# A hybrid encoder layer: output-projection pieces also in the three preparing turns, and at three quarters of the pace in the turns after them

## The chip, the core and the metric

The kernel runs on one core of a Trainium2 chip. The metric is device time in microseconds (us) of one execution of the whole program. Five engines matter: PE (TensorE, matrix products), DVE (VectorE), ACT (ScalarE), POOL (GpSimd) and SP (SyncE), which here issues every DMA of the program in the order of its own queue. Each engine works through its instructions in a fixed order; an instruction that waits holds everything behind it on the same engine.

## The reference

One post-norm encoder layer over 2048 tokens of width 1024 (batch 1):

```
h = layer_norm(x)
proj = h @ w_in
y = concat(ssd_bidir(proj[...]), rwkv7_bidir(proj[...]))   # 512 + 512 wide
h = layer_norm(ALPHA * h + y @ w_out)                      # the output projection
out = layer_norm(ALPHA * h + square(relu(h @ w_fc)) @ w_proj)
```

The two mixers run over the sequence in both directions. The first one (SSD) is a chunked scan. The second one (RWKV-7) carries a 64 x 64 state per head, updated with a decay, a rank-one removal and a rank-one write for each token:

```
s_kk = einsum('dbhvk,dbhk->dbhv', S, kk)
S = S * w - s_kk[..., None] * (kk * a)[..., None, :] + v[..., :, None] * k[..., None, :]
y = einsum('dbhvk,dbhk->dbhv', S, r)
```

The output projection `y @ w_out` is a sum of two products: the SSD half of `y` with the first 512 rows of `w_out`, and the RWKV half with the last 512 rows. The SSD half is complete before the RWKV scan begins; the RWKV half becomes complete token block by token block as the scan from both ends meets.

## The kernel before, in words

The program has three stages. `phase_in` (line 504) normalises `x`, multiplies it with `w_in` and runs most of the element-wise work and the SSD group. `phase_rwkv` (line 926) runs the RWKV scan. `phase_mlp` (line 1322) is the feed-forward part. Large products are made from three products of split operands (high part times high part, high times low, low times high), so one 128 x 512 output block with 4 chunks of 128 rows costs 12 matmuls.

**The scan.** It is cut into 32 units (`U = 2 * UN`): 16 blocks of 128 tokens for each of two pairs of heads, both directions in one unit. Four generators do the work of a unit.

- `prep(u)` (line 972) loads the unit's tensors (`rk`, `bk0`, `E`: lines 987, 989, 991), scales them (DVE, lines 997 and 999), forms the small products (PE, line 1009), transposes (PE, lines 1023 and 1033), and at its end writes the triangular matrices `at` to memory as `ad` (DMA, line 1040).
- `inverse(u)` (line 1042) loads `ad` back in another layout as `la` (DMA, line 1046), inverts 16 x 16 triangular blocks in 15 steps of two small operations each (lines 1055 and 1056), and changes the layout through memory again (`nd`, line 1059, then `ni`, line 1062). For even units its 30 operations are on DVE, for odd units on POOL.
- `merge(u)` (line 1075) joins the 16 x 16 inverses to 64 x 64 ones with four small products on PE (lines 1092, 1099, 1112, 1120), with DVE and ACT between them (lines 1096, 1103 on DVE, 1106, 1117, 1124 on ACT).
- `chain(u)` (line 1126) is the recurrence itself: for each of two halves three dependent products on PE (all on line 1140: `ch<-zv,kr`, `ch<-rs,nm`, `ch<-zv,bkt`), each followed by a copy on ACT or DVE (lines 1149, 1158, 1159, 1168, 1172, 1175), and the output products (lines 1155, 1182).

**The turns.** The loop at the end of `phase_rwkv` makes one turn per unit, from `u = -3` to 31. In turn `u` it weaves `chain(u)` with `finish(u - 1)`, `merge(u + 1)`, `inverse(u + 2)` and `prep(u + 3)`. The turns -3, -2 and -1 have no chain: there the main line is `iter([None] * 12)`, twelve empty steps, and only `prep`, `inverse` and, in turn -1, `merge(0)` are made.

**The output projection.** `out_pieces` (line 775) is a generator, `k.fill`. It yields `DENSE` after each 3 matmuls of a 128 x 512 output block (line 828), so one token block of 128 has 8 pieces. In order it makes: 8 pieces of gate products for the scan's output (line 866), the loading and splitting of the first 512 rows of `w_out` (DMA line 789, ACT 797, POOL 798), the scale rows of the SSD half (one transpose on line 877, a trip through memory on lines 881 and 811), then for 16 token blocks a load (`h` line 805, `yr` line 808, DVE 813, ACT 815, POOL 817), 8 pieces, two DVE operations that add them to `h` (line 831) and a store of `h` (line 838). Then follow 8 more gate pieces, the other half of `w_out`, and 16 token blocks of the RWKV half (DVE line 833), each of which waits until both scans have passed it and until a given turn.

**What sets the pace.** `dense(ins, n)` (line 1064) is called after each product of `merge` and `chain`. It adds `n` times a rate to a credit and pulls pieces while the credit is at least 1. The rate is `R0` before turn 1, `R1` in turns 1 to 17 and `R2` later. With rates of 1 a turn asks for 8 pieces (4 in `merge`, 4 in `chain`), from turn 17 on for 7. A piece that is pulled there may not be placed ahead of the product after which it was pulled.

```
k.credit += n * (R0 if k.u < 1 else R1 if k.u < 18 else R2)
with tc.issue_after(ins.ins):
    while k.credit >= 1:
        p = next(k.fill, END) if next(k.ssd, END) is END else END
```

The final order on each engine is made by the framework's scheduler, which orders the instructions by their priorities and a timing model of its own.

## Time and profile before

| | us |
|---|---|
| median of 3 runs | 3469.87 |
| lowest, highest | 3465.22, 3473.87 |
| the profiled execution, its own time | 3477.84 |
| its span, first to last instruction | 3476.0 |

One execution was profiled; all numbers of views are from it. The scan begins on PE at about 1034.8 us of the span, when the last product of `phase_in` ends, and its last unit ends at about 1985.5 us. By the ends of the units' last output products (line 1182), unit 0 ends at 1132.6, unit 3 at 1229.8, unit 15 at 1536.7, unit 16 at 1562.4 and unit 31 at 1985.5 us. Over the whole span PE is busy 3162.8 us (91%), DVE 2035.9 (59%), ACT 1240.3 (36%) and POOL 975.8 (28%).

The views give a time from the span's start, a duration in us, the engine, the line, the operation with the names of what it writes and reads, and in brackets the idle time of that engine ahead of it with what ended it. Rows marked SPq are DMA issues on the SP queue.

### The profile page before, as it was taken

The page shows a single profiled execution, that of the slowest core. Times are in us where ns is not written, and L with a number is a line of the kernel's source. Part 1 is how long each engine was busy: PE and PEld are TensorE (multiplying, and loading weights), DVE is VectorE, ACT ScalarE, POOL GpSimd, SP SyncE. Part 2 cuts the span into 40 slices and gives each one's busy share as a digit, 9 for nine tenths or more (in the row PEclk, how much of TensorE's full clock was granted, in tenths as well). Part 3 has the DMA queues.
Part 4 walks back from the last instruction along what each step waited for, and adds up shares of the span by engine and source line. Part 5 has one row for each costly group of instructions (what it writes and reads, how often), then busy time and mean ns, then how long its engine had stood idle before and what let it go on. Part 6 is the DMA issues. An engine that isn't in the chain of part 4 may idle for free.

```text
span 3476.0 us, 62902 instructions
## 1 busy us (share of the span) xinstructions
PE 3162.8 (91%) x24551; PEld 2525.6 (73%) x24551; DVE 2035.9 (59%) x4186; ACT 1240.3 (36%) x2574; POOL 975.8 (28%) x1278
## 2 busy tenths in 40 slices
PE   5879989988876888888898889999999999999998
PEld 4767867766765666666666678888888788888886
DVE  7798457767675666565767554444444664444446
ACT  3556323433335454455655531122222222222221
POOL 0352134444553221223454551111111111111113
PEclk9989999999995899986978999999999999999999
DMA  5345356776777666656665552111111331111111
GB/s 206 132 158 179 122 148 190 210 214 189 214 226 198 158 170 157 161 158 171 171 164 156 151 189 91 49 49 46 47 49 49 103 109 49 49 49 49 49 49 61
DMA packets 630137, 446.70 MB, mean 129 GB/s; under 512 B 193456, under 2 KB 553552, under 8 KB 629840
## 3 DMA queue, kind: packets, MB, share of 16 engines
q1 hardware_dynamic: 629840, 442.69, 43.5%
q8 instruction: 193, 3.16, 0.4%
q14 instruction: 104, 0.85, 0.1%
HBM read 295.43 MB, written 147.14 MB: 127 GB/s over the span
## 4 chain that ended last, share of the span: by engine, by line
PE 58%; DMA 13%; DVE 13%; issue 4%; POOL 3%; SPq 2%; ACT 2%; DVEq 0%; POOLq 0%; ACTq 0%
PE ps L1362 7%; PE ps L1363 7%; PE ps L1364 7%; PE ps L1384 6%; PE ps L1382 6%; PE ps L1383 6%; PE psg L828 3%; DMA R<-rows 2%; PE psg L268 2%; PE psg L269 2%; PE psg L270 2%; PE ch L1140 2%; DMA la<-ad 1%; DMA ad<-at 1%; PE ps L1009 1%
## 5 line engine op out<-in xcount | busy, mean ns | idle before, releaser
L1388 DVE TENSOR_TENSOR acc<-acc,ps 128x512 f32<-128x512 f32 x464 | 318.2, 687 | 445.3 <-PE ps L1384 443.0
L1369 POOL TENSOR_TENSOR ul<-r,uh 128x512 fp32r<-128x512 f32 x128 | 171.1, 1338 | 1189.6 <-ACT uh L1368 1189.6
L1364 PE MATMUL ps<-hl,fh 128*128 128x512 f32 x1024 | 401.6, 392 | 0.0
L1363 PE MATMUL ps<-hh,fl 128*128 128x512 f32 x1024 | 401.5, 392 | 0.0
L1362 PE MATMUL ps<-hh,fh 128*128 128x512 f32 x1024 | 397.5, 393 | 0.6 <-DVE h L833 0.4
L1384 PE MATMUL ps<-ph,ul 128*128 128x512 f32 x1008 | 393.3, 390 | 0.0
L1383 PE MATMUL ps<-pl,uh 128*128 128x512 f32 x1008 | 393.0, 390 | 0.0
L1382 PE MATMUL ps<-ph,uh 128*128 128x512 f32 x1008 | 392.8, 390 | 0.0
L268 PE MATMUL psg<-hh,wh 128*128 128x512 f32 x864 | 357.2, 414 | 9.7 <-ACT u L287 8.9
L269 PE MATMUL psg<-hh,wl 128*128 128x512 f32 x864 | 354.8, 411 | 0.0
L270 PE MATMUL psg<-hl,wh 128*128 128x512 f32 x864 | 352.6, 409 | 1.4 <-DVE hl L238 1.4
L1350 ACT CAST ph<-wraw 128x1024 fp32r<-128x1024 f32 x63 | 63.3, 1051 | 531.2 <-PE ps L1384 527.8
L1362 PEld LDWEIGHTS ps<-hh,fh 128*128 128x128 f32 x1024 | 192.1, 188 | 43.6 <-DVE h L833 0.9
L1363 PEld LDWEIGHTS ps<-hh,fl 128*128 128x128 f32 x1024 | 192.3, 188 | 42.6
L1364 PEld LDWEIGHTS ps<-hl,fh 128*128 128x128 f32 x1024 | 192.2, 188 | 42.7
L1383 PEld LDWEIGHTS ps<-pl,uh 128*128 128x128 f32 x1008 | 189.4, 188 | 40.9
L1382 PEld LDWEIGHTS ps<-ph,uh 128*128 128x128 f32 x1008 | 189.1, 188 | 40.8
L1384 PEld LDWEIGHTS ps<-ph,ul 128*128 128x128 f32 x1008 | 189.3, 188 | 40.4
L268 PEld LDWEIGHTS psg<-hh,wh 128*128 128x128 f32 x864 | 169.5, 196 | 49.1 <-ACT u L287 10.1
L270 PEld LDWEIGHTS psg<-hl,wh 128*128 128x128 f32 x864 | 168.4, 195 | 39.6 <-issue 3.2
L269 PEld LDWEIGHTS psg<-hh,wl 128*128 128x128 f32 x864 | 169.3, 196 | 35.7 <-issue 2.3
L1366 ACT ACTIVATE r<-ps 128x512 f32<-128x512 f32 x128 | 76.8, 601 | 291.3 <-PE ps L1364 286.5
(294 smaller groups left out, 6182.6 us busy)
## 6 DMA issues: line engine op xcount, KB each, us to landing
h<-hD SPq DMA_DIRECT2D x64, 512.0 KB, 3.8
wraw<-in_w_fc_dram SPq DMA_DIRECT2D x64, 512.0 KB, 3.9
wraw<-in_w_proj_dram SPq DMA_DIRECT2D x64, 512.0 KB, 4.4
rk<-rk SPq DMA_DIRECT2D x64, 384.0 KB, 4.4
eD<-et SPq DMA_DIRECT2D x32, 514.0 KB, 2.7
E<-eD SPq DMA_DIRECT2D x64, 257.0 KB, 4.4
xs<-xg SPq DMA_DIRECT2D x64, 256.0 KB, 4.1
R<-rows SPq DMA_DIRECT2D x64, 256.0 KB, 4.4
```

The source lines that it names most:

```text
L268: nc.tensor.matmul(pt, wh[:, c], hh[:, c], start=(c == 0), stop=False)
L269: nc.tensor.matmul(pt, wl[:, c], hh[:, c], start=False, stop=False)
L270: nc.tensor.matmul(pt, wh[:, c], hl[:, c], start=False, stop=(c == KC - 1))
L828: nc.tensor.matmul(pt, y, w, start=(i == 0), stop=(i == 11))
L1362: nc.tensor.matmul(pt, wh[:, c], k.hh[:, c, ns], start=(c == 0), stop=False)
L1363: nc.tensor.matmul(pt, wl[:, c], k.hh[:, c, ns], start=False, stop=False)
L1364: nc.tensor.matmul(pt, wh[:, c], k.hl[:, c, ns], start=False, stop=(c == KC - 1))
L1369: nc.gpsimd.tensor_tensor(ul[:, ns], r, uh[:, ns], ALU.subtract)
L1382: nc.tensor.matmul(pt, uh[:, ts], ph[:, hs], start=(i == 0), stop=False)
L1383: nc.tensor.matmul(pt, uh[:, ts], pl[:, hs], start=False, stop=False)
L1384: nc.tensor.matmul(pt, ul[:, ts], ph[:, hs], start=False, stop=(i == len(ops) - 1))
L1388: nc.vector.tensor_tensor(acc[j][:, hs], acc[j][:, hs], pt, ALU.add)
```

## The change

Two edits. The rates `R0` and `R1` go from 1.0 to 0.75, so that a turn from 0 to 16 asks for 6 pieces in place of 8. And a new generator `ramp` takes the place of the twelve empty steps in turns -3, -2 and -1: after each of its 12 steps it pulls one piece, 36 in all, if the SSD generator has nothing left. These pulls are not tied to a product. The counts of instructions on every engine stay the same.

```
-R0 = 1.0
-R1 = 1.0
+R0 = 0.75
+R1 = 0.75
 R2 = 1.0
...
         k.fill = out_pieces(k)
         k.credit = 0.0
+
+        def ramp():
+
+            for _ in range(12):
+                yield
+                if next(k.ssd, END) is END:
+                    for p in k.fill:
+                        if p is DENSE or p is HELD:
+                            break
+
         k.final = [0] * NT
...
-            weave(chain(u) if u >= 0 else iter([None] * 12), jobs)
+            weave(chain(u) if u >= 0 else ramp(), jobs)
```

Three places show how the order moves.

**PE, from the first product of `merge(0)` on.** `ip` is the result of `merge`, `psg` that of a piece; line 866 is a gate piece, line 828 a piece of the projection. Before:

```order
L1092 MATMUL ip<-n_9985,ao 32x32 x32
L866 MATMUL psg<-yh,gh 128x512
L866 MATMUL psg<-yh,gl 128x512
L866 MATMUL psg<-yl,gh 128x512
L1023 MATMUL ps<-cst,bk 128x64 x4
L1099 MATMUL ip<-dd,t_10050 32x32 x32
L866 MATMUL psg<-yh,gh 128x512
L866 MATMUL psg<-yh,gl 128x512
L866 MATMUL psg<-yl,gh 128x512
```

Now:

```order
L1092 MATMUL ip<-n_10238,ao 32x32 x32
L828 MATMUL psg<-woh,yh 128x512
L828 MATMUL psg<-wol,yh 128x512
L828 MATMUL psg<-woh,yh 128x512
L828 MATMUL psg<-wol,yh 128x512
L828 MATMUL psg<-woh,yl 128x512
L828 MATMUL psg<-woh,yh 128x512
L828 MATMUL psg<-wol,yh 128x512
L828 MATMUL psg<-woh,yl 128x512
```

Between this product and the first `ch<-rs,nm` of the chain there were 15 matmuls of pieces, all of gates; now there are 93, all of the projection (24 ahead of line 1099, 48 by its end or behind it ahead of line 1112, 15 ahead of line 1120, 6 behind it). The 8 gate pieces and the transpose on line 877 now stand ahead, between the products of `prep`. In unit 1 PE had 36 matmuls of pieces and has 21 now; in units 4 to 15 it had 24 in each and has 15 to 21, on average 18, now.

**DVE, in a turn of the steady part in which an inverse of an even unit begins.** Line 1055 with 128x15 is the first step of the inverse, which needs `la`; line 1103 is the transpose that the third product of `merge` waits for. Before:

```order
L1096 TENSOR_TENSOR t_12546<-rc,ip 128x256
L999 TENSOR_TENSOR kr<-rk,E 128x2x128 x4
L1055 TENSOR_TENSOR ltmp<-ln,la 128x15
L831 SCALAR_TENSOR_TENSOR h<-h,psg 128x512
L1056 TENSOR_TENSOR ln<-ln,ltmp 128x15
L1055 TENSOR_TENSOR ltmp<-ln,la 128x14
L1103 STREAM_TRANSPOSE n_12608<-ip 128x256
```

Now:

```order
L1168 TENSOR_TENSOR zv<-zz_11992,ch 64x4x64 x2
L1169 TENSOR_TENSOR zz_12600<-zz_11992,ch 128x256
L1103 STREAM_TRANSPOSE n_12720<-ip 128x256
L1084 TENSOR_TENSOR dd<-ni,rc 128x256
L999 TENSOR_TENSOR kr<-rk,E 128x2x128 x4
L1055 TENSOR_TENSOR ltmp<-ln,la 128x15
L831 SCALAR_TENSOR_TENSOR h<-h,psg 128x512
```

The transpose of `merge` now stands ahead of the first step of the inverse. In every second such turn line 999 stands behind that step instead. Between the first and the last step of an inverse on DVE stood 20 other DVE operations and stand 17 or 19 now; inside an inverse on POOL stood one subtraction of line 817 and stands one now in every second.

**SP, in a turn of the steady part in which an inverse on POOL ends.** `nd` and `ni` (lines 1059, 1062) are the way out of one unit's inverse; `ad` and `la` (lines 1040, 1046) are the way into the next unit's. Before:

```order
L1059 DMA nd<-ln 512x1x16
L1193 DMA yaD_125<-ye 128x2x128 x2
L1059 DMA nd<-ln 512x1x16
L989 DMA bk_17295<-bk_106 128x4x128
L987 DMA rk<-rk_105 128x6x128
L1062 DMA ni<-nd 64x8x16 x2
L1040 DMA ad<-at 64x8x64 x2
L989 DMA bk_17370<-bk_107 128x4x128
L1046 DMA la<-ad 64x16x16 x2
```

Now:

```order
L987 DMA rk<-rk_105 128x6x128
L1059 DMA nd<-ln 512x1x16 x2
L989 DMA bk_16465<-bk_106 128x4x128
L1062 DMA ni<-nd 64x8x16 x2
L1040 DMA ad<-at 64x8x64 x2
L989 DMA bk_16529<-bk_107 128x4x128
L1046 DMA la<-ad 64x16x16 x2
```

The store of the chain's output (line 1193) no longer stands between the two `nd`, and one load has moved ahead of them. `ni` stands ahead of `ad`, as before. From the last units of the scan on, the order in the MLP stage is the same but for two of its transposes.

## The prediction

> **What bounds the kernel now.** I read the page first, then windows cut at the ends of units, then the waits of the steady part, then its timeline on four engines. In the windows the columns after the length are busy time of PE, PEld, DVE, ACT and POOL, then the granted TensorE clock, DMA share and GB/s.
>
> ```profile
> 1034.80:1097.30 62.50, 35.12 (x220) 29.08 (x220) 36.91 (x100) 33.39 (x87) 31.02 (x58) 0.54 0.84 228
> 1097.30:1119.40 22.10, 15.98 (x234) 11.88 (x233) 9.06 (x41) 8.80 (x22) 1.75 (x3) 0.52 0.55 124
> 1119.40:1132.60 13.20, 12.92 (x329) 10.46 (x330) 8.22 (x22) 9.74 (x27) 3.62 (x12) 1.00 0.76 209
> 1132.60:1166.80 34.20, 27.21 (x466) 20.75 (x466) 22.02 (x67) 13.69 (x39) 10.48 (x25) 0.85 0.69 179
> 1166.80:1199.40 32.60, 28.79 (x424) 21.40 (x426) 16.76 (x47) 12.79 (x36) 7.85 (x23) 0.69 0.48 120
> 1199.40:1229.80 30.40, 25.17 (x443) 19.77 (x444) 19.84 (x62) 13.69 (x39) 5.47 (x13) 0.89 0.65 173
> 1353.40:1383.10 29.70, 23.83 (x429) 18.36 (x430) 19.24 (x63) 12.57 (x36) 6.22 (x16) 0.89 0.60 160
> 1383.10:1404.40 21.30, 21.05 (x429) 16.36 (x429) 12.44 (x39) 12.59 (x36) 6.65 (x20) 1.00 0.66 164
> 1229.80:1536.70 306.90, 268.24 (x5137) 207.85 (x5138) 190.86 (x601) 151.62 (x433) 77.25 (x210) 0.93 0.62 160
> 1536.70:1985.50 448.80, 392.96 (x6483) 297.89 (x6482) 301.64 (x747) 247.88 (x675) 216.83 (x387) 0.84 0.60 160
> 1170.00:1190.00 20.00, 17.94 (x213) 13.12 (x215) 12.05 (x38) 7.82 (x24) 1.27 (x1) 0.50 0.54 120
> 1985.50:3476.00 1490.50, 1458.89 (x6404) 1194.94 (x6402) 688.70 (x926) 330.36 (x470) 240.75 (x180) 0.99 0.21 69
> ```
>
> The change touches only the scan, 1034.8 to 1985.5. Units 1 to 3 take 97.2 us (34.2 + 32.6 + 30.4). Units 4 to 15 take 306.9 us and alternate: one unit of 21.3 us in which PE never rests and the clock is 1.00, and one of 29.7 us in which PE is idle 5.9 us and the clock is 0.89. A pair is 51.15 us. What makes the odd unit long is in the waits of units 4 to 15 (total, times, longest):
>
> ```profile
> PE ip L1112 <- ACT nm L1106: 28.7, 6, 5.6
> ...
> DVE ltmp L1055 <- DMA la<-ad: 32.1, 6, 6.2
> ```
>
> DVE waits for `la` at each of the six inverses that it begins there, and PE waits behind it, by way of a copy on ACT. Rows of one pair's timeline, picked from the engines' own:
>
> ```profile
> 1363.65 1.30 SPq L1062 DMA_DIRECT2D ni<-nd  x2
> 1365.00 1.31 SPq L1040 DMA_DIRECT2D ad<-at  x2
> 1368.38 1.94 SPq L1046 DMA_DIRECT2D la<-ad  x2
> 1372.45 0.17 DVE L1055 TENSOR_TENSOR ltmp<-ln,la 128x15 f32<-128x15 f32 x1 [5.01 <-DMA la<-ad]
> 1375.45 1.06 PE L1112 MATMUL ip<-n,at 32*32 32x32 f32 x32 [4.38 <-ACT nm L1106]
> 1386.79 1.71 SPq L1059 DMA_DIRECT2D nd<-ln  x2
> 1388.59 1.27 SPq L1040 DMA_DIRECT2D ad<-at  x2
> 1393.08 1.29 SPq L1046 DMA_DIRECT2D la<-ad  x2
> 1397.77 0.21 POOL L1055 TENSOR_TENSOR ltmp<-ln,la 128x15 f32<-128x15 f32 x1 [3.94 <-DMA la<-ad]
> 1399.13 1.28 POOL L817 TENSOR_TENSOR yl<-yr,yh 128x512 fp32r<-128x512 f32 x1
> 1408.42 0.21 POOL L1056 TENSOR_TENSOR ln<-ln,ltmp 128x8 f32<-128x8 f32 x1
> 1409.29 1.09 SPq L1193 DMA_DIRECT2D yaD<-ye  x2
> 1423.18 0.18 DVE L1055 TENSOR_TENSOR ltmp<-ln,la 128x15 f32<-128x15 f32 x1 [4.42 <-DMA la<-ad]
> ```
>
> This is a closed loop, since SP is in order: an inverse ends, its `nd` goes out, the next unit's `ad` stands behind it, `la` behind `ad`, and the next inverse waits for `la`. Its links: inverse on DVE from 1372.45 until its `nd` goes out at 1386.79, 14.3 us; out and in to 1397.77, where POOL too has waited for `la`, 11.0; inverse on POOL to 1408.63, 10.9; out and in to 1423.18, 14.55, the longest because `ni` (which waits for `nd` to land) stands ahead of `ad`. They sum to 50.7, the pair's length. So **the pair is set by this loop, not by PE**, which has 6 us of idle in it. Taking pieces out of PE does not shorten the pair by itself.
>
> **The change part by part.** The price of a piece of 3 matmuls: rows of two neighbouring matmuls in a run, of a single warm piece and what follows it, and of a single cold one and what follows it.
>
> ```profile
> 1366.68 0.39 PE L828 MATMUL psg<-woh,yh 128*128 128x512 f32 x1
> 1366.91 0.40 PE L828 MATMUL psg<-wol,yh 128*128 128x512 f32 x1
> ...
> 1384.01 0.50 PE L828 MATMUL psg<-woh,yh 128*128 128x512 f32 x1
> ...
> 1384.90 0.38 PE L1092 MATMUL ip<-n,ao 32*32 32x32 f32 x22
> ...
> 1098.29 0.80 PE L866 MATMUL psg<-yh,gh 128*128 128x512 f32 x1
> ...
> 1099.86 0.69 PE L1023 MATMUL ps<-cst,bk 64*128 64x64 f32 x4
> ```
>
> In a run a matmul follows the last by 0.23 us, so a piece costs 0.7 us; alone between other work it costs 0.89 warm (1384.01 to 1384.90) and 1.57 cold (1098.29 to 1099.86).
>
> *(a) The ramp, in front of unit 0.* The start of the chain now:
>
> ```profile
> 1097.28 1.07 PE L1092 MATMUL ip<-n,ao 32*32 32x32 f32 x64
> ...
> 1119.42 0.68 PE L1140 MATMUL ch<-rs,nm 64*64 64x64 f32 x16
> ...
> 1145.36 0.80 PE L828 MATMUL psg<-woh,yh 128*128 128x512 f32 x1 [6.95 <-ACT yh L815]
> ...
> h<-hD SPq DMA_DIRECT2D x64, 512.0 KB, 3.8
> ```
>
> The gate pieces go into the window 1034.8 to 1097.3, where PE is idle 27.4 us: 8 x 1.57 = 12.6 us, hidden. Their stores and the scale rows' trip now stand on SP among the loads of `prep` and the first `la`; I take 3 us for it (0 to 8). The projection pieces do not go into that idle time. The order puts 31 of them (93 matmuls) between the first `merge` product and the first `ch<-rs,nm`, a path of 22.1 us that PE holds in order. Removed from it: 5 gate pieces, 7.9 us, and 6.1 us of idle. Left: about 7 us. Added: some 3 us until the first `yh` is there (6.95 was waited before), then 8 pieces cold, 12.6, and 23 warm, 16.1. Together 38.7, 16.6 more. Low: all warm, 31 x 0.7 + 7 = 28.7, 6.6 more. High: all cold, 31 x 1.57 + 7 = 55.7, 33.6 more; the two buffers of `h`, whose every load (3.8 us to landing) waits for a store, would hold it there too. With the 3 us: **+19 (7 to 42)**.
>
> *(b) Units 1 to 3.* The 6.95 us wait is gone; unit 1 has 21 matmuls of pieces in place of 36, and unit 2's cold stretch (1170 to 1190 at clock 0.50, about 9 us lost) had the same start. If the three run at the steady 25.6 us, they take 76.7: **-20**. Low -25, high -8 (only the wait is gone).
>
> *(c) Units 4 to 16.* The loop's links after the change, by the order: 17 or 19 other DVE operations lie inside the inverse on DVE in place of 20, each some 0.35 us (the inverse's own 30 at 0.2 leave 8 of its 14.3 us for the 20), 0.7 us less; in the pairs shown `yaD` no longer stands between the two `nd`, 1.1 less; in every second pair an inverse on POOL has no `yl` inside (1.28 us), 0.64 less on average. Sum -2.5; in some turns `hD` and a `yr` load move ahead of `la`, +0.5. I take -2 per pair, six pairs and unit 16 at half: **-13**. Best: -4, also the 4 freed pieces shorten DVE's part, -26. Worst: the loop unchanged and the clock worse, which is the rival below, +26. PE: 4 pieces fewer, 2.8 to 3.6 us per pair, go into idle that PE has already, and so does DVE's one addition for each 4 pieces. The transpose that `merge` waits for is now ahead of the wait for `la`; late next is the copy `zv` (line 1159), still behind that wait, so the chain stands in its place.
>
> The granted clock after the stall is 0.50 for 6 us and then full:
>
> ```profile
> 1375.40:1381.40 6.00, 5.95 (x84) 4.73 (x86) 4.84 (x20) 2.23 (x6) 0.00 (x0) 0.50 0.60 202
> ```
>
> Here two pieces follow the stall at once. The window 1170 to 1190 shows the other case: PE busy 17.94 of 20 us, and the clock still 0.50. The Trainium skill (TensorE: Matmul & The Clock Gate, "Part 1: The HAM clock gate") says that about 3.4 us of sustained activity lift the throttle; by that a stall would cost under 2 us and the clock rival below would fall away. The first of these windows is near it; the second, 20 us of nearly unbroken small matmuls, does not agree, so the rival keeps its chance.
>
> *(d) Units 17 to 31 and the MLP.* The rate there is unchanged, the pieces are the same, and the 448.8 us have no steady pattern; orders differ by a few rows. 0, with 10 us either way. The MLP, 1490.5 us at 98% PE, keeps its order: 0.
>
> **Sum**: 19 - 20 - 13 = -14 us. From the profiled execution's 3477.84 (span 3476.0) that is 3464; this execution is 8 us above the median of the runs, 3469.87, so against the median **3456**.
>
> **The rivals.** *No gain.* The loop keeps 50.7 us because `ni` still stands ahead of `ad`, and ramp and early units cancel: +19 - 20 = -1, 3469. For it: the idle that PE has in every odd unit. Against it: the DMA row that left the loop. *Slower, by the clock.* With 6 pieces a turn some stalls are followed by no piece for most of a turn; if each pair then has a stretch like 1170 to 1190, PE loses about 9 us where it lost 3, which passes the 6 us of idle: about +4 per pair, 6.5 pairs, +26, with (a) and (b) +25: 3495. It decides once the clock stays at 0.50 for more than some 12 us after each stall. For it: the order has the chain's wait followed by small matmuls only. Against it: a cold stretch also shortens the next stall. *PE sets the pair after all.* Then all 31 + 5 pieces taken from the turns count, 36 x 0.8 = 29: 19 - 20 - 29 = -30, 3440. For it: the even unit has no idle. Against it: the loop sums to the pair.
>
> **How the numbers follow.** Forecast 0.45, no gain 0.25, slower 0.22, PE 0.08. About 0.3%, 10.4 us, can be told from no change here. The forecast and the PE case lie below 3459.5 for most of their spread (b and d alone give it some 15 us), the no-gain case mostly within: faster 0.50, same 0.26, slower 0.24. The forecast's own range is 3440 to 3472; the range with the rivals is 3430 to 3488.
>
> **What would show it.** Right: the first `ch<-rs,nm` 10 to 25 us later; the first projection piece ahead of it; units 1 to 3 at 75 to 80 us; a pair of units near 49 us, with PE idle still some 6 us and DVE and POOL still waiting for `la`. Wrong: a pair that shortens to 46 or less (PE was the bound), a clock below 0.85 in units 4 to 15 (the clock rival), or a ramp over 42 us late that is never won back.

## The result and the profile after

The change takes **3491.93 us** (median of 15 runs, 3483.86 to 3512.81) against 3473.87 (15 runs, 3465.09 to 3494.34) for the kernel before: ratio **1.0056**, interval 1.0036 to 1.0075. Run again it is 3493.98 (12 runs), ratio 1.0039, interval 1.0021 to 1.0058. So it is slower, by 14 to 19 us, where -14 was forecast.

The windows of the changed kernel, cut at the ends of the same stages as in the prediction (columns: busy time of PE, PEld, DVE, ACT, POOL; then granted clock, DMA share, GB/s):

```profile
1034.60:1108.90 74.30, 48.39 (x258) 37.18 (x259) 39.88 (x107) 40.14 (x103) 29.79 (x53) 0.57 0.93 258
1108.90:1146.90 38.00, 30.82 (x299) 23.11 (x299) 20.83 (x65) 6.76 (x15) 9.04 (x12) 0.85 0.58 146
1146.90:1170.20 23.30, 20.68 (x366) 16.36 (x366) 14.75 (x36) 9.60 (x27) 10.20 (x32) 0.73 0.60 162
1170.20:1244.20 74.00, 64.01 (x1254) 50.39 (x1254) 46.47 (x143) 35.80 (x104) 14.39 (x37) 0.87 0.60 148
1244.20:1560.40 316.20, 295.53 (x5494) 231.91 (x5492) 202.24 (x621) 164.85 (x474) 81.99 (x220) 0.90 0.61 154
1560.40:1996.10 435.70, 381.02 (x6061) 287.80 (x6061) 300.35 (x714) 232.17 (x637) 209.24 (x375) 0.83 0.59 155
1996.10:3482.80 1486.70, 1457.97 (x6403) 1193.95 (x6402) 687.88 (x924) 329.38 (x469) 241.22 (x180) 0.99 0.21 69
```

The first three are the ramp and unit 0: 74.3 + 38.0 + 23.3 = 135.6 us, where before it was 62.5 + 22.1 + 13.2 = 97.8. Units 1 to 3 (fourth row) give back 23 us, units 4 to 16 (fifth) 16, units 17 to 31 (sixth) take 13 more, the MLP 4 less. That is +6.8 in this pair of profiled executions (3484.63 against 3477.84). The execution profiled after the change is the second fastest of its 15, the one before lies above its median, so the medians differ by more. To be less at the mercy of one execution, I profiled both once more (runs e4 and f4 below). Stage lengths in us; a unit ends with its last `yp` product of line 1182, and the first two columns count from the end of `phase_in`'s last large product (lines 268 to 270), which itself lay between 1028 and 1045 in all the profiles here, by chance as far as I can see:

| profile | first merge product | unit 0 ends | units 1-3 | units 4-16 | units 17-31 | MLP |
|---|---|---|---|---|---|---|
| before | 62.5 | 97.8 | 97.2 | 332.6 | 423.1 | 1490.5 |
| before again (f4) | 60.9 | 97.8 | 93.6 | 329.5 | 423.5 | 1488.3 |
| change | 74.3 | 135.5 | 74.1 | 316.2 | 435.8 | 1486.7 |
| change again (e4) | 72.4 | 132.5 | 74.5 | 319.8 | 428.8 | 1487.6 |
| mean difference | +11.7 | +36.2 | -21.1 | -13.1 | +9.0 | -2.2 |

The sum of the last five is +8.8. What more the medians show (14 to 19 us) lies in executions that were not profiled: those of the change spread from 3471.68 to 3512.81. Two terms stand out against the forecast: the ramp, +36 where I had +19, and units 17 to 31, +9 where I had 0.

**Why the first merge product is late.** From the timelines of SP, DVE and PE, around `nd` and `ni` of unit 0; first two rows of before, then the changed kernel:

```profile
1087.84 1.48 SPq L1059 DMA_DIRECT2D nd<-ln  x2
...
1092.98 1.29 SPq L1062 DMA_DIRECT2D ni<-nd  x2
```

```profile
1091.66 2.15 SPq L1059 DMA_DIRECT2D nd<-ln  x2
1093.86 2.21 SPq L1046 DMA_DIRECT2D la<-ad  x1
...
1096.87 1.27 SPq L1040 DMA_DIRECT2D ad<-at  x2
...
1101.39 1.28 SPq L1062 DMA_DIRECT2D ni<-nd  x2
...
1107.41 0.43 DVE L1084 TENSOR_TENSOR dd<-ni,rc 128x256 f32<-128x256 f32 x1 [2.80 <-DMA ni<-nd]
...
1108.89 1.08 PE L1092 MATMUL ip<-n,ao 32*32 32x32 f32 x64 [7.02 <-POOL ltmp L1055]
```

Before, `ni` went out 3.7 us behind the end of `nd`'s issue (1087.84 + 1.48 to 1092.98); now nine other transfers are issued between them and it is 7.6. And `ni` needs longer: DVE gets it 6.0 us after its issue. Counted from the end of `phase_in`, `nd` goes out 4.0 us later than before, `ni` 8.6 and the first merge product 11.8, so the delay grows in three steps of about 4 us: ahead of `nd`, between `nd` and `ni`, and behind `ni`. The totals of the DMA view, for the window from the end of `phase_in` to the first merge product, and for `ni` the median time from issue to landing; first of before, then of the change:

```profile
DMA packets 26767, 14.24 MB, mean 228 GB/s; under 512 B 10208, under 2 KB 24713, under 8 KB 26761
...
ni<-nd SPq DMA_DIRECT2D x2, 32.0 KB, 2.3
```

```profile
DMA packets 32888, 19.19 MB, mean 258 GB/s; under 512 B 11986, under 2 KB 29554, under 8 KB 32882
...
gD<-h SPq DMA_DIRECT2D x4, 512.0 KB, 4.0
h<-hD SPq DMA_DIRECT2D x2, 512.0 KB, 6.7
...
ni<-nd SPq DMA_DIRECT2D x2, 32.0 KB, 5.3
```

The pieces brought their transfers with them, 4.95 MB more: four stores of gates and two loads of `h` are 3 MB of it. The 16 DMA engines were 0.84 busy in this window before and are 0.93 now, and 32 KB take 5.3 us to land in place of 2.3. That a full set of DMA engines, and not SP's order, makes the start late is a theory at this point; the runs below test it.

### The profile page after: what moved, and what is told of

It reads as the page before. It is cut to its first block, busy times and chain, and to the rows that moved or that the text cites. A ratio compares the mean times of both kernels' runs of the same rounds, so it can differ in the third digit from the quotient of the medians.

```text
span 3482.8 us, 62842 instructions
## 1 busy us (share of the span) xinstructions
PE 3198.7 (92%) x24551; PEld 2555.8 (73%) x24551; DVE 2058.3 (59%) x4186; ACT 1236.2 (35%) x2574; POOL 977.1 (28%) x1278
## 4 chain that ended last, share of the span: by engine, by line
PE 51%; DMA 7%; DVE 7%; ACT 2%; issue 1%; POOL 1%; SPq 1%; DVEq 0%; POOLq 0%; ACTq 0%
PE ps L1372 7%; PE ps L1374 7%; PE ps L1373 7%; PE ps L1394 6%; PE ps L1392 6%; PE ps L1393 6%; PE psg L828 2%; PE ch L1140 2%; PE ps L1009 2%; DMA la<-ad 1%; DMA yr<-yS 1%; DVE sd L1220 1%; DMA ad<-at 1%; DMA nd<-ln 1%; PE ps L828 1%
## 5 line engine op out<-in xcount | busy, mean ns | idle before, releaser
L269 PEld LDWEIGHTS psg<-hh,wl 128*128 128x128 f32 x864 | 170.5, 197 | 36.2 <-issue 2.3
```

Of the source, the lines that this page charges most:

```text
L269: nc.tensor.matmul(pt, wl[:, c], hh[:, c], start=False, stop=False)
```

## The experiments

Each ratio is against runs of the kernel before on the same chip.

### Each part alone (e1, e2), the gates alone (e3), the change again (e4)

e1 is the change with its first two numbers put back, e2 the kernel before with the two numbers changed, e3 the change with a counter in `ramp` and another pace:

```diff
 e1:  R0 = 1.0, R1 = 1.0          (with ramp)
 e2:  R0 = 0.75, R1 = 0.75        (without ramp)
 e3:  R0 = R1 = 0.97; k.ahead = 8
-                if next(k.ssd, END) is END:
+                if k.ahead and next(k.ssd, END) is END:
+                    k.ahead -= 1
```

> The three preparing turns pull pieces as in the change, but the pace is 1.0 as before (pieces of the first half are then used up about four units earlier). Theory A, the start pays: pieces placed between the first merge product and the first chain product put the end of unit 0 about 37 us later (1132.6 to some 1170), units 1 to 3 give back some 15 to 20, units 4 to 12 keep a pair of 51, so about 15 to 22 us slower than before (ratio 1.004 to 1.007). Theory B, the lower pace costs (fewer pieces, a colder clock in units 4 to 31): with the pace back at 1.0 units 4 to 12 keep their clock of 0.93, only the units without pieces go colder, and the run is within 8 us of before (ratio 0.999 to 1.003).

Measured: 3528.19, ratio 1.0142 (1.012 to 1.0165).

> The pace is 0.75 in units 0 to 17 and nothing is pulled ahead. By the order 24 pieces (72 matmuls) then come after the last unit, about 17 us at 0.23 us a matmul. Theory A: unit 0 ends where it did before (1132.6, within 6), units 1 to 3 take 80 to 90, units 4 to 16 give 16 us as in the change, and the 17 us behind the last unit take that back: 3460 to 3475 against 3474 (ratio 0.996 to 1.001). Theory B: units 4 to 16 gain nothing once they are averaged over runs, units 17 to 31 lose 12, the tail 17: 3495 to 3505 (ratio 1.006 to 1.009).

Measured: 3525.63, ratio 1.0132 (1.0113 to 1.0151).

> The preparing turns pull only the eight gate pieces, no product piece, and the pace is 0.97, so that the first half is used up at the same unit as before. Theory A: first chain product at most 6 us later than before (1119.4 to 1125), the rest of unit 0 at 13 to 16 us and not 23, units 1 to 3 shorter by about 10, and the rest as before: 3462 to 3474 (ratio 0.997 to 1.000). A rival to A, that it is the loads and stores on SP's queue which delay the start whatever the piece is: first chain product 10 to 20 us later and the run 5 to 15 us slower (1.0015 to 1.004).

Measured: 3510.24, ratio 1.0101 (1.0075 to 1.0126).

> The change itself again, for a second profile beside the others. Theory A: unit 0 ends between 1165 and 1175, units 1 to 3 take 72 to 78, units 4 to 16 take 312 to 322, and what varies between profiles lies in units 17 to 31 (430 to 450). Ratio 1.004 to 1.0075. If the 12.6 us that units 17 to 31 lost in the first pair of profiles were chance, they take 420 to 428 here.

Measured: 3493.98, ratio 1.0039 (1.0021 to 1.0058); stages in the table above.

Both theories fell: each part alone is much slower than both together, and a small part of the change (the gates, with nearly the old pace) costs more than the whole. In stages:

| profile | first merge product | unit 0 ends | units 1-3 | units 4-11 | units 12-16 | units 17-31 | MLP |
|---|---|---|---|---|---|---|---|
| before | 62.5 | 97.8 | 97.2 | 204.4 | 128.2 | 423.1 | 1490.5 |
| change | 74.3 | 135.5 | 74.1 | 198.5 | 117.7 | 435.8 | 1486.7 |
| e1, ramp alone | 77.2 | 139.0 | 81.8 | 215.7 | 118.9 | 444.6 | 1488.6 |
| e2, pace alone | 60.5 | 101.8 | 87.6 | 196.0 | 145.9 | 439.8 | 1514.6 |
| e3, gates ahead | 68.5 | 112.4 | 78.4 | 225.7 | 131.9 | 436.1 | 1487.2 |

Three things are in it. First, e2's 24 pieces behind the last unit cost 24 us of MLP time (17 was expected). Second, e1 answers whether PE sets the pair of units. By the order, its units 13 to 16 have no pieces at all; its window there, and the same four units of the change, which have 18 piece matmuls each:

```profile
1490.10:1583.30 93.20, 72.67 (x1622) 61.49 (x1621) 56.66 (x181) 48.82 (x144) 22.51 (x64) 0.78 0.58 146
```

```profile
1464.70:1560.40 95.70, 89.82 (x1696) 70.53 (x1694) 60.69 (x185) 54.33 (x152) 27.08 (x68) 0.93 0.62 157
```

17 us less busy PE, 2.5 us less time than in this profile of the change (the others with the same order on PE there, e4, k1, k2 and s2, took 95.7 to 101.7), and a clock of 0.78 in place of 0.93: without pieces the units go little faster. PE is idle for 20.5 of these 93.2 us. Whether the loop of the prediction holds them then, or the colder clock ate what was saved, e1 does not separate. Third, the same pace gave 196.0 and then 145.9 in e2, where the change had 198.5 and 117.7. What differs from unit 13 on is the order of the work on PE. The order is not written by hand: the framework chooses it when it builds the program, and in the steady part it settles into a cycle. I write one unit's PE stream as a line (RP, UP, ZP the chain's products, m1 to m4 those of `merge`, Y1 and Y2 `yp`, G, T, V those of `prep`, D pieces; with counts, which are matmuls for T, V and D and pairs of matmuls for the others):

```
before, every unit 4 to 14:
T4 RP8 D3 m1 11 Y1 1 V2 G8 Y1 7 UP1 T4 UP7 D3 m1 13 T4 V2 Y2 1 m1 5 ZP8 Y2 7 m1 3 Y1 8 RP8 D6 m2 32 D3 UP8 G8 T4 m3 16 D6 ZP8 Y2 3 m4 16 D3 Y2 5
change, unit 12 (one of a cycle of four):
G5 T4 m1 3 RP8 Y1 8 m1 2 T4 m1 9 V2 m1 1 UP5 G4 UP2 G4 UP1 D2 T4 D1 m1 12 Y2 1 m1 5 ZP8 Y2 2 T4 Y2 1 V2 Y2 4 m2 32 Y1 3 RP8 D6 Y1 5 m3 16 D3 UP8 D3 G3 m4 16 D3 ZP8 Y2 8
e2, unit 14 (33 us a unit in units 12 to 14):
T4 RP8 m1 6 V2 Y1 1 G8 Y1 7 T4 UP8 D3 m1 3 T4 V2 m1 5 Y2 1 ZP8 Y2 7 m1 18 Y1 1 RP8 D6 Y1 6 m2 32 Y1 1 UP8 G4 T4 G4 m3 16 D6 ZP8 Y2 1 m4 16 D3 Y2 7
```

The kernel before has one order for all its steady units, the change another in a cycle of four, e2 leaves the change's cycle behind unit 12, and e3, whose pace is no simple fraction, goes through several and reaches before's only in units 14 and 15. From here on the theory (C) was: the start pays for what is put ahead, and every later stage goes by the order that it happens to get.

### The order put to the test (f1 to f4)

```diff
 f1, the change, with the ramp's pulls ranked behind everything else:
+                with tc.high_priority(offset=-1000):
                     if next(k.ssd, END) is END:
 f2, as e3, but with R0 = R1 = 1.0
 f3, the change, pulling in the first two of the three turns:
-                if next(k.ssd, END) is END:
+                if k.u < -1 and next(k.ssd, END) is END:
 f4, the kernel before, for a second profile
```

> The change, with the pieces of the preparing turns given a lower rank than everything else, so that 47 and not 93 of their matmuls stand ahead of the first product with nm, and 27 move from unit 0 to units 1 and 2. From unit 3 on the order on PE is that of the change. Theory C, the start pays for what stands ahead of the chain: with m1 as late as in the change (72 to 74 us behind phase_in), unit 0 ends 115 to 125 us behind phase_in and not 133 to 136, units 1 to 3 take 80 to 88 for the 27 matmuls that they get, unit 0 to 3 together 200 or less against 207 to 210 in the change and 195 before; the run 5 to 12 us below the change (ratio 1.000 to 1.003). Rival, the work itself and not its place is what costs: units 0 to 3 together stay at 207 to 210 and the run at 1.004 to 1.006.

Measured: 3513.95, ratio 1.0124 (1.0101 to 1.0148). Unit 0 ends at 123.9, units 1 to 3 take 88.4: together 212 us, where the change has 207 to 210. The rival was right: pieces that are taken out of the chain's way come back behind it. The rest of the loss is units 17 to 31:

```profile
1578.50:2037.80 459.30, 393.21 (x6059) 298.77 (x6058) 295.07 (x710) 231.36 (x631) 207.01 (x375) 0.79 0.55 146
```

459 us for the work that took 423 before, with the clock at 0.79. (The execution profiled is the slowest of f1's six, 17.5 us above their median, so part of this is chance.)

> Only the eight gate pieces are pulled ahead and the pace is 1.0 as before; from unit 1 on the order on PE is then row for row that of the kernel before, while the run with 0.97 had mixed orders. Theory C, units 4 to 16 go by which repeating order the program has and not by what was pulled ahead: units 4 to 11 take 202 to 207 (before 204.4; with 0.97 225.7), units 12 to 16 125 to 130, the start is as with 0.97 (unit 0 108 to 114, units 1 to 3 75 to 80), and the run is at 3464 to 3476 (ratio 0.997 to 1.001). Rival, that pulling the gates ahead is what spoils the later units: units 4 to 16 stay near 357 and the run at 1.008 to 1.011.

Measured: 3503.14, ratio 1.0085 (1.0067 to 1.0104). Theory C's test of the steady part came out as it said, and the total did not. Nor is the order that of before throughout, as was expected: by the trace it is so, row for row, in units 4 to 13, and it is new behind them.

```profile
1036.20:1108.70 72.50, 42.15 (x221) 32.72 (x221) 36.21 (x100) 37.52 (x95) 27.92 (x47) 0.57 0.90 256
1232.20:1560.00 327.80, 290.37 (x5522) 225.44 (x5524) 209.20 (x635) 170.10 (x482) 91.81 (x229) 0.93 0.65 167
1560.00:2012.80 452.80, 386.43 (x6075) 293.10 (x6074) 301.04 (x710) 228.00 (x627) 204.70 (x369) 0.79 0.54 142
```

With before's order in ten of them the 13 units take 327.8 (before 332.6 and 329.5) at before's clock of 0.93; with the mixed orders of e3 they took 357.6. But units 17 to 31, whose order is new, take 452.8. And eight gate pieces alone make the first merge product 10 to 12 us late, as the whole ramp does (6 to 8 us in e3).

> The change with pieces pulled only in the first two of the three preparing turns, 24 and not 36; 57 matmuls of pieces then stand ahead of the first product with nm, and the twelve pieces left come in units 16 to 18 and behind the last. The order on PE in units 1 to 3 is the one that the run with the pace alone had in units 12 to 14, which took 33 us each. Theory C: unit 0 at 118 to 127, units 1 to 3 at 85 to 98 because of that order (74 in the change), the whole 10 to 25 us above the change (ratio 1.007 to 1.012). Rival, that those units were slow in the run with the pace alone for another reason than the order: units 1 to 3 at 72 to 80 and the run 5 to 10 us below the change (1.001 to 1.004).

Measured: 3505.7, ratio 1.0111 (1.0087 to 1.0134).

```profile
1157.20:1257.00 99.80, 76.58 (x1265) 60.47 (x1266) 50.61 (x160) 36.20 (x105) 15.67 (x38) 0.73 0.49 122
```

Units 1 to 3 take 33 us each, clock 0.73; with the same number of pieces (18 matmuls a unit) and another order the change needs 74 for the three. That is what theory C expected, but it is a weaker case than it looks. By the traces, PE's order in these three units is, but for a few rows, that of e2's units 13, 14 and 16 (not 12 to 14), and there they took 28.5, 36.6 and 27.1 us; e2's unit 15, with the rows of its unit 13, took 20.7. So a unit's order on PE alone does not fix its time.

> The kernel before again, for a second profile: if the stages are steady from one execution to the next, unit 0 ends 95 to 100 us behind phase_in, units 1 to 3 take 95 to 99, units 4 to 16 330 to 335 and units 17 to 31 420 to 426. What differs by more is chance and no effect of the change.

Measured: 3469.86; the stages repeat within 4 us (table above).

How far an order repeats can be read from all the profiles together. Compared row by row, PE's order in units 1 to 14 is the same in eleven of them (change, e4, k1 to k4, r2 to r4, s1, s2; the later ones are described below), and units 4 to 14 took 265 to 283 us in them, 272.0 on average. In the four with before's order there (before, f4, f2, r1) they took 274 to 278, 275.8 on average.

### The start and the late units (k1 to k4)

```diff
 k1, the change, ni of unit 0 loaded by ACT's queue:
-                nc.sync.dma_start(ni[hsl(h)], ...)
+                (nc.scalar if u == 0 else nc.sync).dma_start(ni[hsl(h)], ...)
 k2, the change, the old pace one unit earlier:
-  k.credit += n * (R0 if k.u < 1 else R1 if k.u < 18 else R2)
+  k.credit += n * (R0 if k.u < 1 else R1 if k.u < 17 else R2)
 k3, the change, with the counter of e3 at 28
 k4, the change, with ten of twelve matmuls of the pieces ahead left out:
-  nc.tensor.matmul(pt, y, w, ...)
+  if k.u >= 0 or i in (0, 11): nc.tensor.matmul(pt, y, w, ...)
```

> The change, with the load of ni for unit 0 issued by ACT and not by SP; the order on PE stays that of the change from the first row to the last. Theory C: the load goes out right behind nd's landing, some 4 us earlier, and the first merge product at 69.5 to 72.5 us behind phase_in (change 72.4 and 74.3); unit 0 then ends 1 to 4 us earlier (129 to 134), the run is 0 to 4 us below the change (ratio 1.003 to 1.006). Rival, that it is the inverse of unit 0 or POOL that holds the first merge product: it stays at 72.4 to 74.3.

Measured: 3493.83, ratio 1.0057 (1.0037 to 1.0078). The first merge product comes at 71.9, 0.5 to 2.4 us earlier than in the change. ACT issues the load as soon as `nd` has landed, 62.7 us behind `phase_in` in place of 64.4 to 66.8, but it lands later after its issue: the row, and `ni`'s time to landing in the DMA view.

```profile
1107.63 1.35 ACTq L1062 DMA_DIRECT2D ni<-nd  x2
...
ni<-nd ACTq DMA_DIRECT2D x2, 32.0 KB, 5.5
```

So the place of `ni` in SP's order is worth some 2 us of the 11.7 at most. The Trainium skill bears on this (DMA: Bandwidth & Descriptors, "Issuing engines are not separate DMA queues"): transfers that different engines issue share the same 16 DMA engines, and another issuer saves the time to issue only. The 5.5 us agrees.

> The change, but the pace goes back to 1.0 one unit earlier (at unit 17), which adds one piece to unit 17; the order on PE is that of the change up to unit 16 and another one in units 17 to 31. Theory C, that units 17 to 31 go by the order that they happen to get: stages up to unit 16 as in the change within 6 us, units 17 to 31 outside of 426 to 438 (other orders took 423 to 459), the run off the change by as much. Rival, that pace and pieces set them: 427 to 437, ratio 1.004 to 1.007.

Measured: **3475.29**, ratio **0.9998** (0.9984 to 1.0013). One number, which the change had left as it was, takes the whole loss away. Units 4 to 16, units 17 to 31, and units 17 to 21 alone; then units 17 to 21 of the change:

```profile
1244.80:1564.60 319.80, 296.67 (x5494) 233.03 (x5494) 201.02 (x622) 164.86 (x475) 82.25 (x220) 0.90 0.60 152
1564.60:1986.10 421.50, 360.53 (x6061) 272.81 (x6061) 299.28 (x712) 230.74 (x633) 209.57 (x374) 0.85 0.60 161
1564.60:1711.00 146.40, 125.76 (x2137) 94.84 (x2137) 104.62 (x261) 87.64 (x244) 69.06 (x134) 0.85 0.69 181
```

```profile
1560.40:1722.00 161.60, 138.77 (x2137) 107.17 (x2138) 102.64 (x268) 87.58 (x243) 67.69 (x135) 0.76 0.63 166
```

The start is the change's (unit 0 ends at 135.7), units 4 to 16 too; units 17 to 31 take 421.5 and not 436, with the same 6061 matmuls in 20 us less busy PE. Their clock is 0.85 and not 0.83. The difference arises in units 17 to 21, which have the same number of matmuls on PE in both: 146.4 us (148.1 in k2's second profile, s2) against 161.6 (156.1 to 159.6 in the three others with the change's order there, e4, k1 and k4), with the clock at 0.85 (0.80 in s2) and not 0.76.

> The change with 28 pieces pulled ahead and not 36 (8 gate and 20 projection pieces); the order on PE in units 1 to 14 is that of the change, another one later, and nothing more is left behind the last unit. Theory C: 24 matmuls fewer ahead of the chain, at 0.23 to 0.36 us each 6 to 9 us: unit 0 ends 124 to 129 behind phase_in, units 1 to 3 take 73 to 76, units 4 to 11 196 to 203; if units 17 to 31 took 432 again, the run would be 6 to 9 us below the change (1.002 to 1.004). Rival, that transfers and not matmuls fill the start: unit 0 still ends at 131 to 136.

Measured: 3481.55, ratio 1.003 (1.0013 to 1.0048). Unit 0 ends at 127.4, 7 us earlier for 8 pieces fewer, and no more pieces are left behind the last unit; units 17 to 31 took 436.5.

> Left out: ten of every twelve matmuls of the projection pieces that are pulled ahead (78 of 129 projection matmuls in unit 0), so that what they compute is incomplete; their loads, evacuations and stores stay, and so does the order on every row of PE but those and one late unit. Theory C: the start is paid in PE time, 78 matmuls at 0.23 to 0.36 us: unit 0 ends 18 to 28 us earlier, 106 to 117 behind phase_in, units 1 to 31 as in the change, ratio 0.997 to 1.001. Rival, that transfers (the h loads and stores, SP's queue) fill the start: unit 0 ends at 125 or later, ratio 1.003 or more.

Measured: 3481.96, ratio 1.0028 (1.0008 to 1.0048). Unit 0 ends at 126.1, only 8 us earlier. Its three windows:

```profile
1035.70:1106.80 71.10, 43.85 (x256) 33.94 (x256) 40.29 (x107) 39.50 (x103) 29.45 (x52) 0.60 0.96 270
1106.80:1127.30 20.50, 14.37 (x218) 9.41 (x218) 15.39 (x47) 6.51 (x15) 7.85 (x12) 0.50 0.69 171
1127.30:1161.90 34.60, 26.78 (x368) 20.31 (x368) 19.46 (x54) 10.00 (x28) 11.81 (x34) 0.53 0.65 170
```

This splits the start. The first merge product hardly moves (71.1, in the change 72.4 and 74.3), so little of its lateness is the pieces' matmuls. From there to the first product with `nm` it is 20.5 and not 38.0: that part is the matmuls, 17.5 us for 78 of them, 0.22 each. But the rest of unit 0 then takes 34.6 and not 23.3 (20.8 in e4), with the clock at 0.53 and not 0.73: without the long matmuls PE stays at about half clock here, and gives 11 of the 17 us back.

### Transfers added and taken away (r1, r2), and two smaller ramps (r3, r4)

```diff
 r1, the kernel before, behind each load of E in the first three prep:
+   with tc.issue_after(ins.ins):
+       for i in range(2):
+           dum = k.dr.tile([P, 770], F32, name=f"dum{...}")
+           nc.sync.dma_start(dum, k.cst[:, 0:770])
 r2, the change, without h for the pieces ahead:
-   nc.sync.dma_start(h, k.hD[t])
+   if not first or k.u >= 0: nc.sync.dma_start(h, k.hD[t])
+   (and for these pieces h = pt in place of ALPHA * h + pt)
 r3, r4: k3 with R1 up to unit 17 and up to unit 16 (k.u < 17, k.u < 16)
```

> The kernel before, with twelve stores of 394 KB each (4.7 MB) from a constant to scratch memory added on SP's queue in the three preparing turns, spread behind the loads of prep; nobody reads them. The order on PE in units 4 to 17 is that of before. Theory D, the preparing window is bound by the DMA engines (0.84 busy before, 14.3 MB in 62.5 us; 19 MB in 72 to 74 us in the change): the first merge product comes 70 to 78 us behind phase_in in place of 61 to 62.5, the DMA share of the window is 0.93 or more, unit 0 ends 106 to 113 behind phase_in. Rival, transfers are hidden and the gate pieces' compute or SP's order made the start late: first merge product at 60 to 64, unit 0 at 96 to 100.

Measured: 3507.87, ratio 1.0114 (1.0072 to 1.0155).

> Left out: the loads of h for the projection pieces that are pulled ahead (512 KB each, two of them ahead of the first merge product) and the adding of h to what those pieces compute; the order on PE is that of the change up to unit 17. Theory D: 1 MB less ahead of the first merge product is 4 us at 258 GB/s, so it comes at 67 to 71 (change 72.4 and 74.3), and the evacuations no longer wait for a load, so unit 0 ends 122 to 130 (change 132.5 and 135.5). Rival: no change in the first merge product (72 to 74) and in unit 0 (132 to 136).

Measured: 3502.26, ratio 1.0095 (1.006 to 1.013). The window up to the first merge product in r1, then in r2:

```profile
1035.10:1113.40 78.30, 37.26 (x235) 30.15 (x237) 39.64 (x116) 34.48 (x94) 26.40 (x51) 0.53 0.98 260
```

```profile
1032.40:1102.00 69.60, 41.67 (x256) 32.29 (x255) 40.69 (x107) 39.24 (x103) 29.93 (x54) 0.64 0.93 256
```

r1 has no piece ahead, only 4.7 MB more to move, and its first merge product comes at 78.3 in place of 61 to 62.5; unit 0 ends at 114.1, 16.3 us later. r2 moves 17.8 MB (69.6 us at 256 GB/s) in place of 19.2, and is 2.8 to 4.7 us earlier than the change's two profiles, though only 1.4 earlier than k3. The lateness goes with the bytes, roughly:

| | MB in the window | us to the first merge product | DMA share |
|---|---|---|---|
| before, f4, e2 | 14.2 to 14.4 | 60.5 to 62.5 | 0.84, 0.85 |
| r2 | 17.8 | 69.6 | 0.93 |
| e3, f2 (gates only) | 18.6 | 68.5, 72.5 | 0.96, 0.90 |
| f1 | 18.9 | 70.2 | 0.95 |
| change, e1, e4, f3, k1 to k4, r3, r4, s1, s2 | 19.1 to 19.2 | 71.0 to 77.2 | 0.91 to 0.97 |
| r1 | 20.4 | 78.3 | 0.98 |

(The MB are the window's length by its GB/s.) From 17.8 MB on, the engines moved 0.25 to 0.27 MB/us in every one of these kernels. That more transfers make the start late is shown: transfers alone do it (r1). That fewer of them undo some of it (r2), and fewer matmuls less (k4), fits, within a few us. The bytes are not the whole price, though: r1's 4.7 MB are 18 us at 260 GB/s, of which the free 0.16 of before's 62.5 us could take ten, and it came 16 to 17 us later and not 8. That it is the engines' share and not the places in SP's queue, which every transfer takes too, is what k1 and the landing times point to; it was not separated further. r2's unit 0 still ends at 134.6: theory D (that the DMA engines bind the preparing window) was right on the first merge product and wrong on the rest, of which, by k4, a part is PE's own time. In r1, as in f2, the late units lost too (436.9, another order again), and so did r2's (units 4 to 16 334.1 with the change's order, units 17 to 31 444.2 with another). From unit 20 to 28, f2, r1 and r2 have the same order on PE but for a few rows: units 21 to 28 took 252.5, 250.9 and 252.8 us.

> 28 pieces ahead as in the run with 28, and the pace back to 1.0 at unit 17; the order up to unit 14 is that of the run with 28, another one behind unit 15. Unit 0 to 16 as there (unit 0 126 to 130, units 1 to 3 73 to 76, units 4 to 16 310 to 320). Units 17 to 31 can't be told ahead: 421 to 445 by the orders seen so far, the run 0.997 to 1.004 of before; below 0.9985 it would beat both kernels.

Measured: 3482.84, ratio 1.0025 (1.0002 to 1.0048); units 17 to 31 433.7.

> The same with the pace back to 1.0 at unit 16, a third late order. Unit 0 to 15 as in the run with 28, units 17 to 31 somewhere in 421 to 445, the run 0.997 to 1.004 of before. If r3 and r4 differ by more than 6 us in units 17 to 31, with the same pieces in the same number, the order alone is worth that much there.

Measured: 3491.31, ratio 1.0052 (1.0032 to 1.0073); units 17 to 31 435.2. Two more late orders, no gain, and no difference between them beyond 6 us. The medians are 8 us apart though the two profiles are not: r3's profile is of the slowest of its ten executions.

### The late units once more (s1, s2)

s1 is k2 with `k.u < 16`; s2 is k2 again.

> The change with the pace back to 1.0 at unit 16, two units earlier: the same 36 pieces ahead, the order of the change up to unit 16, a third order in units 17 to 31. If those units go by their order: units 0 to 16 as in the change within 6 us, units 17 to 31 at neither 432 nor 421.6, and the run apart from the change by as much. If it was the one piece more in unit 17 that helped in the run with unit 17, this one, which has the same pieces there or more, is at 418 to 425 and 0.998 to 1.001 too.

Measured: 3489.69, ratio 1.0043 (1.0022 to 1.0064).

> The run with the pace back at unit 17 again, for a second profile: units 17 to 31 at 418 to 425 if the 421.6 belongs to its order, 427 or more if it was chance; first merge product 71 to 74 behind phase_in and unit 0 133 to 137 as before.

Measured: 3464.22 in one execution. Units 4 to 16 and 17 to 31, first of s1, then of s2:

```profile
1240.90:1577.30 336.40, 309.36 (x5509) 243.19 (x5508) 210.19 (x626) 168.11 (x481) 88.89 (x231) 0.86 0.59 150
1577.30:2000.90 423.60, 366.60 (x6045) 278.22 (x6045) 288.28 (x707) 227.72 (x627) 204.35 (x364) 0.85 0.59 156
```

```profile
1238.10:1559.40 321.30, 295.43 (x5492) 231.81 (x5494) 203.43 (x622) 165.27 (x475) 82.49 (x220) 0.90 0.59 151
1559.40:1971.70 412.30, 355.27 (x6061) 269.92 (x6061) 301.46 (x712) 230.33 (x633) 210.62 (x375) 0.87 0.62 165
```

k2's order gave 421.6 and 412.4 in two profiles; the change's order gave 435.8, 428.8 and, in k1 and k4, whose PE order there is the same (in k4 but for one unit), 429.6 and 436.5. The groups do not overlap, and the medians agree with them (0.9998 against 1.0056, 1.0039 and 1.0057), so the 421.6 was not chance alone. The 412.4 partly is: s2's one execution was faster than all twelve of k2. s1's third order gave 423.6. That a piece more in unit 17, and not the order, helped k2 is unlikely by the traces: between the ends of units 16 and 17 it has 9 piece matmuls, as the change has, and s1 has 3. And r3, which differs from k3 by the same edit as k2 from the change, has 21 piece matmuls there where k3 has 15, and took 433.7 for 436.5. What in the order is worth the 16 us stays open. s1 also shows how unsteady the change's cycle is: its units 4 to 16 took 336.4 where the change took 316.2, with the same PE order up to unit 15 (units 4 to 15 306.8 against 293.5).

No run beat the kernel before. The nearest, k2, is as fast as it is, within 0.16% either way.

## Why the prediction was wrong

**The ramp, (a): mis-sized, +36 and not +19.** It was made of three parts. *The first merge product 3 us later (0 to 8)* was the step that failed: it is 11.7 later. I put the gate pieces into a window "where PE is idle 27.4 us: hidden", and costed their transfers as places in SP's queue. The row that I quoted for that window says DMA share 0.84. PE had room there and the DMA engines had little: 4.95 MB at 258 GB/s are 19 us, of which the free 0.16 of 62.5 us could take ten, which leaves 9. r1 bears out that transfers alone delay it, k4 that the matmuls do not; how the delay divides between bytes and places in SP's queue stays open. *The path from there to the first `ch<-rs,nm`, 38.7 us,* came out at 38.0 and 39.3, and k4 shows that 17.5 of them are the matmuls. But the sum was right by luck: 22.1 - 7.9 - 6.1 is 8.1 and not "about 7", most pieces ran warm and not eight of them cold, and a stall of 5.88 us is in it that the forecast did not have:

```profile
1123.58 0.76 PE L828 MATMUL psg<-woh,yh 128*128 128x512 f32 x1 [5.88 <-DVE h L831]
```

It is not the wait for a load of `h` of the high case: r2, which loads none there, has the same stall, 5.49 us. DVE comes late to line 831, which stands in its order behind steps of an inverse and behind a row of line 813 at 1120.85, which had waited 0.94 us for a load of `yr`. *The rest of unit 0* I did not cost at all: 23.3 and 20.8 us in place of 13.2 and 14.6, the clock at 0.73 and 0.84 in place of 1.00 and 0.88.

**Units 1 to 3, (b): right.** -21 against -20. That they run at the steady pace hung on the order too: with the same pieces in other places they took 99.8 in f3.

**Units 4 to 16, (c): the size by luck, the mechanism not shown.** -13.1 in two profiles against -13, but over the six profiles with the change's start and its PE order (change, e4, k1, k2, s2, s1: 316.2 to 336.4) the mean is 323.2, 8 below before, and over the eleven profiles that share the order of units 4 to 14 these are 4 below. "They sum to 50.7, the pair's length. So the pair is set by this loop" proves less than it says: stretches that run from one start of an inverse on DVE to the next such start add up to the pair whatever sets it. That PE alone does not set it is what its idle time and e1 say. The pairs of units 4 to 15 take 48.9 us on average in the first profile, near the 49 of the forecast. What I had not seen is that the steady pattern itself would go: the order became a cycle of four units whose clock is 0.90 and not 0.93, and whose length varies by 20 us from one profile to the next, where before's repeats within 5 (with f2 and r1).

**Units 17 to 31, (d): put at nothing, and wrong.** "The rate there is unchanged, the pieces are the same ... orders differ by a few rows. 0." (The 448.8 us of the prediction include unit 16; units 17 to 31 took 423.1.) None of the fifteen units has the sequence of rows on PE that it had before. By order and chance together, these units took between 412 and 459 us with nearly the same work, and the change drew an order that costs 9. k2 draws another, and with everything else of the change in place the loss is gone. In its two profiles the stages are +36 - 21 - 11 - 6 (417.0 against 423.3) + 0 = -2 us against before, which fits its ratio of 0.9998.

**The rivals.** "Slower, by the clock" had the time, 3495, and not the reason: the clock in units 4 to 16 did fall, from 0.93 to 0.90, but these units got shorter, not 26 us longer. Its ramp and early units were the forecast's, 19 - 20 = -1; they came to +15, and that, with units 17 to 31, made up the time. "PE sets the pair", by which every piece taken out counts, does not fit e1, where 17 us less PE work saved 2.5. "No gain" had the loop unchanged, which it is not.

**What was to show it.** The first projection piece ahead of the first `ch<-rs,nm`, units 1 to 3 near 75 and a pair near 49 all came; that product 27 us later and not 10 to 25 was the sign that the ramp was too small in the sum. PE's idle in a pair is 3.4 us and not 6. Waits of units 4 to 15 (total, times, longest), one of before and three of the changed kernel:

```profile
POOL ltmp L1055 <- DMA la<-ad: 22.3, 6, 5.1
```

```profile
DVE ltmp L1055 <- DMA la<-ad: 13.7, 5, 3.6
...
PEld ip L1112 <- ACT nm L1106: 0.5, 2, 0.3
...
POOL ltmp L1055 <- DMA la<-ad: 33.9, 6, 6.7
```

DVE's waits for `la` have shrunk from 32.1 us to 13.7, and POOL's have grown from 22.3 to 33.9. PE's wait for `nm` behind DVE's, 28.7 us before, no longer stands among PE's waits, and 0.5 us is left of it at the weight load (PEld) of the same product. That fits the transpose, which now stands ahead of the wait for `la`; the prediction named this move and gave it no time of its own. Still the pairs are only 2 us shorter: PE was busy 5 us more in these twelve units, with some 70 matmuls fewer and the clock at 0.90 in place of 0.93.

## What to carry to other kernels

Before work is moved into a window, read the DMA share of that window as well as the idle time of the engine: pieces bring their loads and stores, and in a window with a share of 0.84 it was these, and hardly the matmuls, that set what the gate pieces cost. Where a scheduler lays out the order, a small edit can redraw it far behind the edit; a stage without a steady pattern is then no "0", but a draw whose width should be in the range (here 412 to 459 us, chance included). And one profile of one execution is a draw too: with the same order, units 4 to 14 took 265 to 283 us. When each part alone is slower than all of them together, look for what each of them disturbs besides its own work.

## What the runs showed of the hardware

**In unit 0 long matmuls brought the clock up, and without them it stayed down.** Windows of the changed kernel at the start of its pieces:

```profile
1110.00:1113.40 3.40, 3.34 (x8) 2.67 (x9) 2.86 (x6) 0.01 (x1) 3.16 (x6) 0.52 0.70 168
1113.50:1117.20 3.70, 3.70 (x17) 2.82 (x15) 2.71 (x8) 0.62 (x1) 1.31 (x2) 1.00 0.43 97
1117.70:1123.50 5.80, 0.00 (x0) 0.00 (x0) 4.59 (x17) 0.62 (x1) 1.65 (x2) 0.71 0.45 81
1123.60:1126.60 3.00, 3.00 (x7) 2.42 (x8) 2.66 (x14) 0.00 (x0) 0.00 (x0) 0.50 0.51 52
1126.80:1146.00 19.20, 18.00 (x169) 13.02 (x168) 6.93 (x18) 4.91 (x12) 2.59 (x2) 1.00 0.66 194
```

The clock goes from 0.52 to 1.00 after 3.4 us of unbroken 512-wide matmuls, falls to 0.50 in a stall of 5.9 us, and is back after 3.2. The Trainium skill's rule (TensorE: Matmul & The Clock Gate, "Part 1: The HAM clock gate") of about 3.4 us of sustained activity agrees here. In the prediction's window 1170 to 1190, with PE busy 17.94 of 20 us on small matmuls, and in k4's 55 us at 0.50 and 0.53, it hardly lifted: a high busy share in the profile is not enough for it, and what more it takes no run here shows. So a matmul left out can cost time: with 78 fewer, the rest of unit 0 took 34.6 us and not 23.3.

**The DMA engines were nearly full at 248 to 271 GB/s.** In the window up to the first merge product their share was 0.90 to 0.98 in every kernel that moved 17.8 MB or more, and in the change 11986 of 32888 packets were under 512 B. The Trainium skill (DMA: Bandwidth & Descriptors, "Specifications") has about 358 GB/s for one core's share of HBM and says that transfers under 512 B do not reach line rate. The measured rate is 24 to 31% below its figure; that the small packets are why was not tested.
